# Two heads in alternation on half-filled array tiles, and an ordering model with other costs

## The chip, the cores and the metric

One core of one Trainium2 chip. The metric is device time in microseconds (us) of one execution; the kernel before has a median of 3313.85 us over 3 runs (3313.74 to 3313.91). TensorE (PE) multiplies, VectorE (DVE), ScalarE (ACT) and GpSimd (POOL) work on rows of 128 partitions, SyncE (SP) issues transfers. PEld is TensorE's weight load, which overlaps with its products.

## The reference

512 tokens of width 1024 pass through two blocks of two layers each. The first block's layer: RMS norm, one input projection, two attentions side by side, gated sum, output projection, and a gated FFN. Windowed attention (stage A below): 8 query heads of width 64 in 2 kv groups, query blocks of 128 tokens against a band of the neighbouring blocks, a sink column in the softmax. Neighbourhood attention (stage B): 8 heads on an 8 x 64 grid, query blocks of 16 grid columns against 32.

```python
scores = einsum('bnqkgd,bnjkd->bnkgqj', qb, kb) * HEAD_DIM ** -0.5     # windowed, 4 heads g to one kv head k
p = softmax(concatenate([where(valid, scores, NEG), sink_col], -1))[..., :-1]
out = einsum('bnkgqj,bnjkd->bnqkgd', p, vb)
...
scores = einsum('brjqhd,brjwkhd->bhrjqwk', qg, kb) * HEAD_DIM ** -0.5  # neighbourhood
p = softmax(scores + bias)
out = einsum('bhrjqwk,brjwkhd->brjqhd', p, vb)
```

The second block has retention, a gated linear recurrence and a convolution as mixers, a convolutional FFN and layer norms; no line of its computation is edited.

## The kernel before, in words

Every operand that needs float32 precision is held as a high and a low part in a short format (tiles `hi`, `lo`, and `whi`, `wlo` for weights), and a product is three: hi x hi, lo x hi, hi x lo into the same PSUM tile (`mm3`, line 658; `proj_a` 664 and `proj_b` 680 for weights, 128x512 each, tile `ps`). Attention weights `pe` and values `va` are multiplied in plain float32.

The program is first recorded on virtual tiles (`Recorder.add`, line 349): each operation with its tiles, its predecessors and the engines that may do it. Most have one; `any_tt` may go to VectorE or GpSimd, `any_copy` to ScalarE or VectorE. `order` (line 408) is a list scheduler: it keeps a clock for each engine, takes the first operation in program order that is ready within a window of 3000, prices it by `_cost` (line 289), makes its successors ready a fixed `HOP` of 0.25 us after its end on another engine, and gives a two-way operation to the engine that would end it sooner. Tiles come from lanes with a fixed number of slots; lane `p` is the 8 banks of PSUM. A free slot can be taken again `HOP` after its last use. `issue` (line 581) then issues the operations to the engines' queues in that order, so each queue is what the model made it, and all instructions carry line 603.

In stage A, `attn_a_block` (line 897) runs over one block of 128 queries: for each of the two kv heads, four score tiles `s` (one for each query head of the group; the head width of 64 fills partitions 0 to 63 or 64 to 127, `pr`), the mask and maximum on VectorE, the exponentials on ScalarE, the scaling on VectorE, then per key block four transposes into `pt`, a copy `pe`, and the value product into the rows `pr` of the one output tile `o`, which means 64 of the array's columns. Its four blocks have 2, 3, 3 and 2 key blocks. In stage B, `attn_b_block` (line 984) runs over four blocks of grid columns and four pairs of heads; the two heads of a pair have one row half each. The copies there are `peb` and, of the values, `vb`; the transposes are `ptb` and `vtp`.

The layer norms of the second block (`ln_start` to `ln_end`, lines 1192 to 1233) sum tiles by `any_tt`: `lns`, `lnq`, and `x` times its row factor `spread`.

Of the kernel before, what the change touches and what calls it, by code (L numbers as in the profile page):

```python
# [18 lines left out]
P = 128  # L19
# [18 lines left out]
# ---------------------------------------------------------------- host layout  # L38

def _units_a(w, cols):  # L40
    """Column tiles of w as stationary blocks: [tile, 128, K/128 * 128]."""
    k = w.shape[0] // P
    out = []
    for c in cols:
        out.append(w[:, c].reshape(k, P, len(c)).transpose(1, 0, 2).reshape(P, -1))
    return np.stack(out)


def _units_b(w, cols):
    """A group of columns of w as moving blocks: [unit, 128, kk * len(cols)], 1024 wide."""  # L50
# [161 lines left out]
HOP = 0.25  # L212
# [20 lines left out]
class View:  # L233
    """A tile, a stand-in with its shapes, and the steps that lead to the view from the tile."""
# [19 lines left out]
    def box(self):  # L254
        """Partitions and range of the free dimensions; a whole tile in PSUM."""
# [21 lines left out]
class Op:  # L277
    __slots__ = ("i", "prio", "ways", "args", "kw", "tiles", "new", "npred", "succ", "ready", "done", "start", "cost", "urgent", "columns")
# [10 lines left out]
def _cost(eng, name, args, kw):  # L289
    """Microseconds that the engine is held."""  # L290
    out = kw["out"] if "out" in kw else args[0]
# [11 lines left out]
    if eng == "ACT":  # L303
        return (0.051 if ps else 0.093) + 0.093 * aps + n * 0.000833 + (0.05 if "accum_out" in kw else 0)
    if eng == "POOL":
        return 0.146 + n * 0.00211
# [22 lines left out]
class Recorder:  # L329
# [19 lines left out]
    def add(self, ways, name, args, kw):  # L349
# [5 lines left out]
        if "out" not in kw and isinstance(args[0], View):  # L355
# [17 lines left out]
        ins += [v for v in (args if "out" in kw else args[1:]) if isinstance(v, View)]  # L373
# [23 lines left out]
        if ways == ("PE",):  # L397
            op.columns = outs[0].size * (2 if name == "transpose" else 1 if args[2].ap.dtype == F32R else 4)
# [8 lines left out]
    # -- the order  # L407
    def order(self):
# [30 lines left out]
        def safe(t):  # L439
            """The rest can still run in program order when t takes a slot now."""  # L440
# [30 lines left out]
        while n_sched < len(ops):  # L471
# [17 lines left out]
            while avail[e]:  # L489
# [15 lines left out]
                wait, hold = now, None  # L505
                for t in op.new:
# [3 lines left out]
                    if not sl or not safe(t):  # L510
                        hold = t.lane
                        break
                    wait = max(wait, sl[0])
# [23 lines left out]
            else:  # L537
# [6 lines left out]
                if e == "PE":  # L544
# [3 lines left out]
                    rows = op.args[1].shape[0]  # L548
                    clock[tick] = clock.get(tick, 0.0) + op.columns * rows / P
# [4 lines left out]
            for sp, data in op.succ:  # L554
                same = len(sp.ways) == 1 and sp.ways[0][0] == e
                sp.ready = max(sp.ready, fin + (HOP if not same else SAME if data and e != "PE" else 0.0))
# [3 lines left out]
            for t in op.tiles:  # L560
                t.left -= 1
                t.busy = max(t.busy, fin)
                if t.left == 0 and t.lane in LANES:
                    live[t.lane].discard(t)
                    heapq.heappush(slots[t.lane], t.busy + HOP)
# [15 lines left out]
    def issue(self, tc, order):  # L581
        nc = tc.nc
        engs = {"PE": nc.tensor, "ACT": nc.scalar, "DVE": nc.vector, "POOL": nc.gpsimd, "SP": nc.sync}
        with ExitStack() as ctx:
# [8 lines left out]
            with tc.manual_schedule():  # L593
                for op, e, name, kw in order:
# [7 lines left out]
                    r = lambda v: v.resolve() if isinstance(v, View) else v  # L602
# [1073 lines left out]
```

## Time and profile before

| | |
|---|---|
| median of 3 runs | 3313.85 us (3313.74 to 3313.91) |
| the profiled execution's span | 3312.1 us; its time is this and about 1.75 us around it, by the median of the runs |
| TensorE busy | 3265.5 us, 99%, 16096 instructions |
| VectorE, ScalarE, GpSimd busy | 2117.9 (64%), 1203.7 (36%), 178.2 (5%) us |
| granted TensorE clock | full in all 40 slices of the page |

A row of the timeline with x2 holds two instructions of one kind that start together or one behind the other; the duration is from the first start to the last end. Ends of products are modelled and reach beyond the next start, since products are pipelined: what one costs is the distance between starts. The chip's row names a tile without its number: `s` is any score tile.

### The profile page before, as it was taken

The page shows a single profiled execution, that of the slowest core. Times are in us where ns is not written, and L with a number is a line of the kernel's source. Part 1 is how long each engine was busy: PE and PEld are TensorE (multiplying, and loading weights), DVE is VectorE, ACT ScalarE, POOL GpSimd, SP SyncE. Part 2 cuts the span into 40 slices and gives each one's busy share as a digit, 9 for nine tenths or more (in the row PEclk, how much of TensorE's full clock was granted, in tenths as well). Part 3 has the DMA queues.
Part 4 walks back from the last instruction along what each step waited for, and adds up shares of the span by engine and source line. Part 5 has one row for each costly group of instructions (what it writes and reads, how often), then busy time and mean ns, then how long its engine had stood idle before and what let it go on. Part 6 is the DMA issues. An engine that isn't in the chain of part 4 may idle for free.

```text
span 3312.1 us, 41658 instructions
## 1 busy us (share of the span) xinstructions
PE 3265.5 (99%) x16096; PEld 2701.6 (82%) x16096; DVE 2117.9 (64%) x4317; ACT 1203.7 (36%) x1947; POOL 178.2 (5%) x142
## 2 busy tenths in 40 slices
PE   8999999999999999999999999999999999999998
PEld 6778888887778888888888888888888788888887
DVE  8777766646655544349984457664599954576644
ACT  5543332224543333223332335442333322354431
POOL 1000000000000000000020001000100200010000
PEclk9999999999999999999999999999999999999999
DMA  4345556641133322332212222233232122322331
GB/s 140 112 155 185 197 180 195 187 143 52 64 115 102 95 96 94 94 104 91 83 58 82 90 89 90 96 95 94 73 103 84 56 81 91 96 83 96 96 92 61
DMA packets 99414, 347.16 MB, mean 105 GB/s; under 512 B 11280, under 2 KB 14224, under 8 KB 99216
## 3 DMA queue, kind: packets, MB, share of 16 engines
q1 hardware_dynamic: 99216, 344.51, 32.6%
q8 instruction: 126, 2.06, 0.3%
q14 instruction: 72, 0.59, 0.1%
HBM read 342.36 MB, written 2.10 MB: 104 GB/s over the span
## 4 chain that ended last, share of the span: by engine, by line
PE 93%; DVE 5%; ACT 1%; issue 0%; DMA 0%; POOL 0%; SPq 0%; DVEq 0%; ACTq 0%; POOLq 0%
PE ps L603 87%; PE hs L603 1%; PE o L603 1%; PE s L603 1%; DVE x L603 1%; DVE wlo L603 1%; PE pt L603 1%; DVE scb L603 0%; PE ho L603 0%; PE ro L603 0%; ACT scb L603 0%; PE rs L603 0%; DVE cacc L603 0%; DVE rs_t L603 0%; DVE hw L603 0%
## 5 line engine op out<-in xcount | busy, mean ns | idle before, releaser
L603 PE MATMUL ps<-hi,whi 128*128 128x512 f32 (+1 forms) x3852 | 1466.8, 381 | 4.2 <-ACT hi L603 2.1
L603 PE MATMUL ps<-hi,wlo 128*128 128x512 f32 (+1 forms) x3852 | 1464.6, 381 | 0.8 <-DVE wlo L603 0.8
L603 PE MATMUL ps<-lo,whi 128*128 128x512 f32 (+1 forms) x3852 | 1464.7, 380 | 0.4 <-POOL lo L603 0.4
L603 ACT CAST whi<-raw 128x1024 fp32r<-128x1024 f32 (+1 forms) x540 | 561.2, 1040 | 1442.4 <-PE ps L603 1030.7
L603 DVE TENSOR_TENSOR wlo<-raw,whi 128x1024 fp32r<-128x1024 f32 (+1 forms) x540 | 658.1, 1220 | 553.5 <-ACT whi L603 541.9
L603 PEld LDWEIGHTS ps<-hi,whi 128*128 128x128 f32 x3852 | 726.6, 189 | 140.0 <-ACT whi L603 3.6
L603 PEld LDWEIGHTS ps<-lo,whi 128*128 128x128 f32 x3852 | 728.0, 189 | 134.0 <-issue 1.4
L603 PEld LDWEIGHTS ps<-hi,wlo 128*128 128x128 f32 x3852 | 728.0, 189 | 133.4 <-DVE wlo L603 1.0
L603 PE MATMUL ps<-whi,hi 128*128 128x512 f32 (+1 forms) x512 | 198.0, 388 | 9.4 <-ACT whi L603 9.4
L603 PE MATMUL ps<-wlo,hi 128*128 128x512 f32 (+1 forms) x512 | 197.4, 386 | 0.0
L603 PE MATMUL ps<-whi,lo 128*128 128x512 f32 (+1 forms) x512 | 197.3, 385 | 0.0
L603 DVE SCALAR_TENSOR_TENSOR cacc<-cu,vez,cacc 128x511 f32<-128x511 f32 (+21 forms) x240 | 165.6, 733 | 0.3
L603 DVE TENSOR_TENSOR g<-ps,spread 128x512 f32<-128x512 f32 x76 | 52.5, 691 | 154.7 <-PE ps L603 152.0
L603 DVE CUSTOM_DVE_ANT_0 raw<-raw,cond 128x512 f32<-128x512 f32 x192 | 128.1, 696 | 9.6 <-DMA raw<-in_wada 9.6
L603 DVE SCALAR_TENSOR_TENSOR cv<-ps,vez,cv 128x510 f32<-128x510 f32 (+1 forms) x176 | 130.2, 745 | 2.7
L603 PEld LDWEIGHTS ps<-whi,hi 128*128 128x128 f32 x512 | 97.1, 190 | 29.0 <-ACT whi L603 9.4
L603 PEld LDWEIGHTS ps<-whi,lo 128*128 128x128 f32 x512 | 97.3, 190 | 18.8 <-issue 1.3
L603 PEld LDWEIGHTS ps<-wlo,hi 128*128 128x128 f32 x512 | 97.4, 190 | 18.1 <-issue 1.0
L603 DVE TENSOR_TENSOR t<-ps,spread 128x512 f32<-128x512 f32 x44 | 30.4, 692 | 113.8 <-PE ps L603 113.8
L603 DVE SCALAR_TENSOR_TENSOR g<-g,ps 128x512 f32<-128x512 f32 x80 | 55.0, 687 | 47.3 <-PE ps L603 46.9
L603 POOL TENSOR_TENSOR lnq<-lnq,lsq 128x512 f32<-128x512 f32 (+1 forms) x22 | 40.0, 1819 | 735.6 <-ACT lsq L603 735.5
L603 ACT ACTIVATE hi<-g 128x512 fp32r<-128x512 f32 x76 | 48.1, 633 | 86.4 <-DVE g L603 80.6
(310 smaller groups left out, 2892.1 us busy)
## 6 DMA issues: line engine op xcount, KB each, us to landing
raw<-in_wada SPq DMA_DIRECT2D x96, 512.0 KB, 4.1
raw<-in_wup SPq DMA_DIRECT2D x88, 512.0 KB, 3.7
raw<-in_wgt SPq DMA_DIRECT2D x48, 512.0 KB, 3.7
raw<-in_wg SPq DMA_DIRECT2D x44, 512.0 KB, 3.8
raw<-in_wu SPq DMA_DIRECT2D x44, 512.0 KB, 3.8
raw<-in_wo SPq DMA_DIRECT2D x32, 512.0 KB, 3.7
raw<-in_wd SPq DMA_DIRECT2D x32, 512.0 KB, 3.6
raw<-in_wdn SPq DMA_DIRECT2D x32, 512.0 KB, 3.5
```

The source lines that it names most:

```text
L603: getattr(engs[e], name)(*[r(a) for a in op.args], **{k: r(v) for k, v in kw.items()})
```

## The change

Two things. First, a recorded operation `group`: several products as one unit in the scheduler's eyes, issued one behind the other, with the members of two lists taken in turn (`side`, `mm3s`). Score products and value products of two heads become such groups in `attn_a_block` and `attn_b_block`: the two heads stand on different row halves (scores) or column halves (values) of the array. In `attn_a_block` all eight score tiles of a block are now made first, then both softmaxes, and per key block both kv heads' transposes and copies come before the pair of value products. A group may take several PSUM slots at once. Second, the scheduler's numbers: `HOP` by the engine that ends and `TO` by the one that starts, `SLOT` for the reuse of a slot, other costs of PE, ACT and POOL. Comments and docstrings are removed. What is computed stays the same.

```diff
-HOP = 0.25
+HOP = {"PE": 0.21, "ACT": 0.14, "DVE": 0.13, "POOL": 0.1, "SP": 0.05}
+TO = {"PE": 0.06, "ACT": 0.0, "DVE": 0.0, "POOL": 0.11, "SP": 0.05}
+ACCUM = 0.1
+SLOT = 0.25
+LOAD = 0.1113
...
-            return 0.11
+            return LOAD
...
-            return max(n, cols) / 2400 + 0.003
-        return 4 * max(n, cols) / 2400 + 0.006
+            return max(n / 2400 + 0.0134, LOAD)
+        return 2 * max(2 * n / 2400 + 0.002, LOAD * cols / P)
...
-        return 0.146 + n * 0.00211
+        return 0.15 + n * 0.0029
...
+                    if name == "group":
+                        for a in op.args:
+                            nc.tensor.matmul(*[r(x) for x in a[:3]], start=a[3], stop=a[4])
+                        continue
...
+    def side(self, groups, cost):
+
+        self.r.tensor.group(*[m for ms in zip(*groups) for m in ms], cost=cost)
+
+    def mm3s(self, out, ahi, alo, bhi, blo):
+        return [(out, ahi, bhi, True, False), (out, ahi, blo, False, False), (out, alo, bhi, False, True)]
...
+        for g in range(4):
+            s = [self.ps([P, nk], "s") for _ in range(2)]
+            self.side([self.mm3s(s[kv], *[a[pr, t * P:(t + 1) * P] for a in qT[g]],
+                                 *[a[pr, kbs[0] * P:kbs[0] * P + nk] for a in kT])
+                       for kv, pr in enumerate(heads)], 3 * max(nk / 2400 + 0.0134, 2 * LOAD))
...
-                pt = self.ps(name="pt")
-                for g in range(4):
-                    r.tensor.transpose(pt[:, g * P:(g + 1) * P], sc[g][:, j * P:(j + 1) * P], self.ident)
-                pe = self.m(name="pe")
-                v.any_copy(pe, pt)
-                r.tensor.matmul(o[pr, :], va[:, kb, pr], pe, start=(j == 0), stop=(j == len(kbs) - 1))
...
+        for j, kb in enumerate(kbs):
+            pes = []
+            for kv in range(2):
...
+                pes.append(pe)
+            self.side([[(o[pr, :], va[:, kb, pr], pes[kv], j == 0, j == len(kbs) - 1)]
+                       for kv, pr in enumerate(heads)], 4 * S / 2400 + 0.43)
```

Groups stand at line 630 of the changed kernel, everything else at 632. The issue order moves at three places of the first layer. Names carry a running number: `s_773` is the score tile of one head, and the two operands behind the arrow are the query's and the key's part.

TensorE's queue at the scores of the first query block of stage A, before: `s_773` is a head of the first kv group, `s_788` and `s_794` are heads of the second.

```order
L603 MATMUL s_773<-hi_739,hi_603 128x256
L603 MATMUL s_773<-lo_755,hi_603 128x256
L603 MATMUL s_773<-hi_739,lo_628 128x256
L603 MATMUL ps_639<-wlo_536,hi_151 128x512
L603 MATMUL ps_639<-whi_436,lo_168 128x512
L603 MATMUL ps_649<-whi_436,hi_151 128x512
L603 MATMUL ps_649<-wlo_536,hi_151 128x512
L603 MATMUL s_788<-hi_739,hi_576 128x256
L603 MATMUL s_788<-lo_755,hi_576 128x256
L603 MATMUL s_788<-hi_739,lo_593 128x256
```
After, at the first of these scores: `s_744` is a head of the first kv group, `s_745` of the second, and so are `s_756` and `s_757`.

```order
L630 MATMUL s_744<-hi_727,hi_568 128x256
L630 MATMUL s_745<-hi_727,hi_568 128x256
L630 MATMUL s_744<-lo_735,hi_568 128x256
L630 MATMUL s_745<-lo_735,hi_568 128x256
L630 MATMUL s_744<-hi_727,lo_584 128x256
L630 MATMUL s_745<-hi_727,lo_584 128x256
L630 MATMUL s_756<-hi_727,hi_577 128x256
L630 MATMUL s_757<-hi_727,hi_577 128x256
```
What stood head by head here, with projections between the two kv groups, now stands product by product in turn.

TensorE's queue at the value products of the second query block, before: `o_1047` is the block's output tile; `pe_1024`, `pe_1043`, `pe_1053` are the weights of the first kv group, the other three of the second.

```order
L603 MATMUL o_1047<-pe_1024,va_616 64x512
L603 MATMUL o_1047<-pe_1043,va_616 64x512
L603 MATMUL o_1047<-pe_1053,va_616 64x512
...
L603 MATMUL ps_626<-whi_517,lo_200 128x512
L603 MATMUL o_1047<-pe_1077,va_616 64x512
L603 MATMUL o_1047<-pe_1088,va_616 64x512
L603 MATMUL o_1047<-pe_1093,va_616 64x512
L603 MATMUL s_1109<-hi_739,hi_603 128x384
```
After: `o_1145` is the same block's output; of each pair the first stands for the first kv group.

```order
L632 MATMUL pt_1133<-ident_106,sc_932 128x128
L630 MATMUL o_1145<-pe_1090,va_617 64x512
L630 MATMUL o_1145<-pe_1130,va_617 64x512
L630 MATMUL o_1145<-pe_1094,va_617 64x512
L630 MATMUL o_1145<-pe_1138,va_617 64x512
L630 MATMUL o_1145<-pe_1098,va_617 64x512
L630 MATMUL o_1145<-pe_1150,va_617 64x512
L630 MATMUL s_1167<-hi_727,hi_595 128x384
```
The value products, which came in two runs of three, one kv group each, now come in one run of three pairs.

TensorE's queue at the first scores of stage B, before: the two heads of the first pair as two blocks of three.

```order
L603 MATMUL s_1900<-hi_1777,hi_1542 128x256
L603 MATMUL s_1900<-lo_1785,hi_1542 128x256
L603 MATMUL s_1900<-hi_1777,lo_1550 128x256
L603 MATMUL s_1906<-hi_1777,hi_1542 128x256
L603 MATMUL s_1906<-lo_1785,hi_1542 128x256
L603 MATMUL s_1906<-hi_1777,lo_1550 128x256
```
After: the same six products in turn.

```order
L630 MATMUL s_1900<-hi_1775,hi_1448 128x256
L630 MATMUL s_1901<-hi_1775,hi_1448 128x256
L630 MATMUL s_1900<-lo_1782,hi_1448 128x256
L630 MATMUL s_1901<-lo_1782,hi_1448 128x256
L630 MATMUL s_1900<-hi_1775,lo_1471 128x256
L630 MATMUL s_1901<-hi_1775,lo_1471 128x256
```
Here the same six products stand next to each other in both orders, and only their turn changes.

## Rows read from the trace of the kernel before

**Rows 1.** the page's summary: busy time, share of the span, instructions
```profile
span 3312.1 us, 41658 instructions
...
PE 3265.5 (99%) x16096; PEld 2701.6 (82%) x16096; DVE 2117.9 (64%) x4317; ACT 1203.7 (36%) x1947; POOL 178.2 (5%) x142
```

**Rows 2.** the page's chain that ended last, share by engine
```profile
PE 93%; DVE 5%; ACT 1%; issue 0%; DMA 0%; POOL 0%; SPq 0%; DVEq 0%; ACTq 0%; POOLq 0%
```

**Rows 3.** stretches: length, busy us (instructions) by engine, granted clock, DMA share, GB/s
```profile
61.56:172.20 110.64, 110.63 (x523) 78.45 (x523) 84.32 (x299) 60.35 (x155) 0.00 (x0) 1.00 0.32 101
172.20:199.00 26.80, 24.15 (x240) 17.73 (x239) 25.40 (x124) 20.39 (x72) 0.00 (x0) 1.00 0.43 136
212.00:720.00 508.00, 508.00 (x2251) 420.83 (x2250) 336.52 (x628) 155.41 (x196) 8.16 (x5) 1.00 0.57 183
786.80:895.80 109.00, 109.00 (x523) 78.03 (x522) 68.40 (x239) 55.60 (x143) 0.00 (x0) 1.00 0.12 39
895.80:922.70 26.90, 24.20 (x240) 17.82 (x239) 25.45 (x124) 20.40 (x72) 0.00 (x0) 1.00 0.38 124
```

**Rows 4.** TensorE's timeline, first layer's stage A: start us, us, what
```profile
98.31 0.40 PE L603 MATMUL ps<-wlo,hi 128*128 128x512 f32 x1
98.64 0.39 PE L603 MATMUL s<-hi,hi 64*128 64x256 f32 x1
...
99.54 0.49 PE L603 MATMUL ps<-whi,lo 128*128 128x512 f32 x1
99.97 0.39 PE L603 MATMUL s<-hi,hi 64*128 64x256 f32 x2
...
100.53 0.50 PE L603 MATMUL ps<-whi,hi 128*128 128x512 f32 x1
```

**Rows 5.** the same view, earlier in that stage
```profile
91.63 2.79 PE L603 MATMUL o<-pe,va 128*64 128x512 f32 x6
94.35 0.45 PE L603 MATMUL s<-hi,hi 64*128 64x384 f32 x2
...
94.98 0.33 PE L603 MATMUL s<-hi,hi 64*128 64x384 f32 x1
...
95.60 0.50 PE L603 MATMUL ps<-whi,hi 128*128 128x512 f32 x1
```

**Rows 6.** stretches, of the instructions on the score tiles s alone
```profile
61.56:172.20 110.64, 16.99 (x96) 13.21 (x97) 15.06 (x32) 1.00 0.32 101
786.80:895.80 109.00, 16.42 (x96) 12.74 (x96) 15.10 (x32) 1.00 0.12 39
```

**Rows 7.** stretches, of the instructions on the output tiles o alone
```profile
61.56:172.20 110.64, 18.88 (x40) 4.82 (x40) 3.80 (x16) 3.45 (x16) 1.00 0.32 101
786.80:895.80 109.00, 18.02 (x40) 4.60 (x40) 3.72 (x16) 3.35 (x16) 1.00 0.12 39
```

**Rows 8.** TensorE's timeline, second layer's stage A
```profile
838.43 1.93 PE L603 MATMUL o<-pe,va 128*64 128x512 f32 x6
840.29 0.66 PE L603 MATMUL pt<-ident,sc 128*128 128x128 f32 x4
```

**Rows 9.** VectorE's groups in 61.56:172.2: busy us, mean ns, idle before
```profile
L603 DVE COPY pe<-pt 128x512 f32<-128x512 f32 x5 | 3.4, 687 | 1.1 <-PE pt L603 1.1
```

**Rows 10.** TensorE's timeline, second layer's stage B
```profile
895.82 0.39 PE L603 MATMUL s<-hi,hi 64*128 64x256 f32 x2
896.04 0.29 PE L603 MATMUL s<-lo,hi 64*128 64x256 f32 x2
```

**Rows 11.** weight loads' waits in 172.2:199: us in total, times, longest
```profile
PEld ptb L603 <- DVE scb L603: 2.7, 6, 0.9
```

**Rows 12.** stretches at a layer norm of the second block, one of three
```profile
2369.00:2376.00 7.00, 4.07 (x32) 3.58 (x30) 6.73 (x9) 5.10 (x10) 5.76 (x5) 1.00 0.38 118
2376.00:2382.80 6.80, 5.92 (x27) 5.92 (x28) 6.67 (x29) 2.77 (x7) 0.82 (x1) 0.50 0.33 112
```

**Rows 13.** GpSimd's groups in 1990:2940
```profile
L603 POOL TENSOR_TENSOR x<-x,spread 128x256 f32<-128x256 f32 x9 | 12.7, 1426 | 17.3 <-DVE spread L603 12.3 <-ACT spread L603 5.0
```

More of the change, by code (lines that the diff above doesn't have):

```diff
@@ L277 @@
 class Op:
-    __slots__ = ("i", "prio", "ways", "args", "kw", "tiles", "new", "npred", "succ", "ready", "done", "start", "cost", "urgent", "columns")
+    __slots__ = ("i", "prio", "ways", "args", "kw", "tiles", "new", "npred", "succ", "ready", "done", "start", "cost", "urgent", "columns", "rows")
 def _meet(a, b):
@@ L354, in add @@
         outs = [kw[k] for k in ("out", "accum_out") if isinstance(kw.get(k), View)]
-        if "out" not in kw and isinstance(args[0], View):
+        if name == "group":
+            views = [v for a in args for v in a[:3]]
+            outs = [a[0] for a in args]
+        elif "out" not in kw and isinstance(args[0], View):
             outs.append(args[0])
@@ L372, in add @@
         ins = [v for k, v in kw.items() if isinstance(v, View) and k not in ("out", "accum_out")]
-        ins += [v for v in (args if "out" in kw else args[1:]) if isinstance(v, View)]
+        if name == "group":
+            ins = [v for a in args for v in a[1:3]]
+        else:
+            ins += [v for v in (args if "out" in kw else args[1:]) if isinstance(v, View)]
         if name == "copy_predicated":
@@ L397, in add @@
         if ways == ("PE",):
-            op.columns = outs[0].size * (2 if name == "transpose" else 1 if args[2].ap.dtype == F32R else 4)
+            op.rows = (args[0] if name == "group" else args)[1].shape[0]
+            if name == "group":
+                op.columns = sum(a[0].size * (1 if a[2].ap.dtype == F32R else 4) for a in args) / 2
+            else:
+                op.columns = outs[0].size * (2 if name == "transpose" else 1 if args[2].ap.dtype == F32R else 4)
         op.tiles = list(al.values())
@@ L509, in order @@
                     sl = slots[t.lane]
-                    if not sl or not safe(t):
+                    k = sum(x.lane == t.lane for x in held)
+                    if len(sl) <= k or not safe(t):
                         hold = t.lane
                         break
-                    wait = max(wait, sl[0])
+                    wait = max(wait, heapq.nsmallest(k + 1, sl)[k] if k else sl[0])
+                    held.append(t)
+                    live[t.lane].add(t)
+                for t in held:
+                    live[t.lane].discard(t)
                 if hold is not None:
@@ L547, in order @@
                         cost *= 2
-                    rows = op.args[1].shape[0]
-                    clock[tick] = clock.get(tick, 0.0) + op.columns * rows / P
+                    clock[tick] = clock.get(tick, 0.0) + op.columns * op.rows / P
                 fin = start + cost
@@ L555, in order @@
                 same = len(sp.ways) == 1 and sp.ways[0][0] == e
-                sp.ready = max(sp.ready, fin + (HOP if not same else SAME if data and e != "PE" else 0.0))
+                if same:
+                    hop = SAME if data and e != "PE" else 0.0
+                else:
+                    hop = HOP[e] + TO[sp.ways[0][0]] + (ACCUM if "accum_out" in kw else 0.0)
+                sp.ready = max(sp.ready, fin + hop)
                 sp.npred -= 1
@@ L564, in order @@
                     live[t.lane].discard(t)
-                    heapq.heappush(slots[t.lane], t.busy + HOP)
+                    heapq.heappush(slots[t.lane], t.busy + SLOT)
                     lst = by_lane[t.lane]
@@ L926, in attn_a_block @@
             for g in range(4):
[L927 removed]
+                r.scalar.activation(out=sc[kv][g], in_=sc[kv][g], func=AF.Exp, scale=rs[:, g:g + 1],
                                     bias=nm[:, g:g + 1], accum_out=den[:, g:g + 1])
@@ L1017, in attn_b_block @@
             v.any_copy(pe, pt)
[L1018 to L1023 removed]
+            self.side([[(o[b * HD:(b + 1) * HD, j * P:(j + 1) * P],
+                         vA[vt[kb]][:, (2 * j + b) * HD:(2 * j + b + 1) * HD],
+                         pe[:, (b * 2 + kb) * P:(b * 2 + kb + 1) * P], kb == 0, kb == 1) for kb in range(2)]
+                       for b in range(2)], 8 * LOAD / 2)
         c0 = jb * 16
```

45 lines of the change are left out of this document (20 added, 25 removed).

## The prediction, on record before the changed kernel ran

> **What bounds the kernel now.** I read the page first. TensorE is busy for 3265.5 of 3312.1 us, 99%, and VectorE for 64% [rows 1]; the chain that ended last is TensorE for 93% of its length and VectorE for 5% [rows 2]. So a microsecond taken off TensorE's own work is a microsecond off the kernel, unless VectorE is late at that place. The table by stretches then shows where the edited code stands: the windowed attention (stage A) of the two layers at 61.56:172.2 and 786.8:895.8, and the front of the neighbourhood attention (stage B) at 172.2:199 and 895.8:922.7 [rows 3]. In A TensorE never idles (110.63 of 110.64) and VectorE is at 76% and 63%. In B it is the other way round: VectorE is busy for 25.40 of 26.80 us, TensorE for 24.15. The yardstick of all ordinary work is its line 212:720, 2251 products of 128x512 in 508.00 us: 0.226 us each.
>
> **Part 1: the scores of stage A.** A score product has 64 contraction rows and so uses half of the array. The rows of the timeline give two prices. Between 98.64 and 99.54 six products of one half, 128x256, take 0.90 us. Between 99.97 and 100.53 six products stand, in the lines marked x2, as three pairs of the two halves, and take 0.56 [rows 4]: three products' time is saved, 0.34/3 = 0.113 each. A run of twelve has three pairs more and takes 0.56 + 0.34 = 0.90. For 128x384 the run 94.35 to 95.60 has three pairs (0.63 us, to 94.98) and then three single products (0.62) [rows 5]: six in pairs take about 0.72 with the edge behind them.
> Before: TensorE's score time in A is 16.99 us in the first layer and 16.42 in the second, 96 products each [rows 6]. The issue order puts them in 15 and 14 runs, and each run's last end lies some 0.07 us behind the next instruction's start (99.34 + 0.28 against 99.54), so 15.94 and 15.44 lie on the path. After: both layers have three runs of twelve and two of six of the 128x256 kind and eight runs of six of the 128x384 kind, all in pairs: 3 x 0.90 + 2 x 0.56 + 8 x 0.72 = 9.6. Saved: 6.3 and 5.8.
>
> **Part 2: the value products of stage A.** Each is 128 rows by 64 columns, half of the array's columns, in plain float32, and stands as two passes in the trace (20 products, 40 records [rows 7]). Six passes one behind the other take 94.35 - 91.63 = 2.72 us [rows 5]. At one place the last product of one kv head is followed by the first of the other, and six passes take 840.29 - 838.43 = 1.86 [rows 8]: two of the six went beside two others. So a slot is (2.72 - 1.86)/2 = 0.43 and a run has 2.72 - 6 x 0.43 = 0.14 on top. Before: 40 slots and 8 runs, 17.2 + 1.12 = 18.3, which is the 18.88 of rows 7 less the tails; the second layer's 18.02 less its tails is 17.5. After: 20 slots, in 5 and 4 runs: 8.6 + 0.7 = 9.3 and 9.2. Saved: 9.0 and 8.3.
>
> **Part 3: the edges.** Where the array goes from full to half products or back, a product takes more than 0.226: 0.33 with one such edge behind it (98.31 to 98.64), 0.43 with one on each side (99.54 to 99.97) [rows 4]: 0.10 each. In the issue orders stage A has 42 and 40 such edges before and 28 in each layer after: 26 x 0.10 = 2.6 saved. With these prices, 253 full products and 133 transposes at 0.11, the first layer's stage adds up to 110.5 of the traced 110.64, so nothing large is missing.
> Parts 1 to 3: 6.3 + 5.8 + 9.0 + 8.3 + 2.6 = 32.0 us of TensorE time that nothing hides.
>
> **Part 4: what is late next in A.** The stage shrinks to about 94 us, and VectorE's 84.32 and 68.40 us of work grow a little: of the copies of transposed weights the new order gives it 15 in the two layers where it had 10, 0.69 us each [rows 9], some 1.7 us a layer. So it stands at 92% in the first layer and 75% in the second. All eight score tiles of a block are now made before the first softmax, and a value pair waits for two copies where a product waited for one; behind that wait on TensorE's queue stand the next projections and, through them, the next scores. Cover is there: the new order draws projection products forward into the stage (141 and 140 of them stand between its first score and its last value product, where 55 and 48 did). If the waits come through, the bound is B, where VectorE at 95% leaves TensorE 2.65 of 26.8 us idle, 10% [rows 3]: 0 to 8 us for the first layer. I take 2.5 + 0.5 = 3.0 lost, near the lower end, since TensorE lost nothing in A at 76%.
>
> **Part 5: stage B.** The diff alternates two heads here too, but the trace of before has them side by side already: the order issues three products of one head and then three of the other, and the timeline shows hi,hi of both at 895.82 and lo,hi of both at 896.04 [rows 10]. So alternation as such buys nothing here. What waits in B is the transpose behind VectorE's scaled scores, 2.7 us in 6 waits [rows 11], and the new order puts two large copies out of PSUM per layer, the 0.69 us kind, on ScalarE that were VectorE's. Bounds: all of TensorE's 2.65 idle us per layer, or as much again lost; I take 2 gained each, 4.0, nearer to the gain because VectorE, which holds the stage up, has less to do.
> Here a rule is weighed. The rows show two heads' products starting together though they were queued as blocks. The Trainium skill, TensorE: Matmul & The Clock Gate, Part 3 ("The mechanism"), says that only weight loads are pulled ahead and that matmuls start and end in strict order; by it blocks would run one after the other, and alternation would halve the 96 score products of B as well. By the rows B gains nothing there. I go by the rows and keep the rule as a rival.
>
> **Part 6: the rest.** The model's new costs (GpSimd dearer, waits between engines shorter) re-order everything behind. GpSimd loses 64 additions, VectorE gets 54 instructions, ScalarE 10; DMA issues on the sync queue move with the order, and no DMA is on the chain [rows 2]. It can matter at the three layer norms of the second block: at the one shown TensorE idles 2.93 us while GpSimd is busy 5.76, and then runs 6.8 us at a granted clock of 0.50, the 1.2 GHz level [rows 12]; one 128x256 addition takes GpSimd 1426 ns [rows 13]. But VectorE, which now does these, is busy 6.73 of those 7.00 us itself. Bounds: three times 2.93 + 3.4 gained, 19 us, or 2 us lost at each, 6. I take 3.0 gained, one idle spell out of three.
>
> Sum: -32.0 + 3.0 - 4.0 - 3.0 = -36.0 from the span of 3312.1 gives 3276.1; the profiled execution's time is its span plus 1.75 us to the median of the runs, 3313.85, so the forecast is 3278 us. Its own range, with parts 4 to 6 a few us either way, is 3268 to 3292.
>
> **Rivals.**
> 1. VectorE becomes the bound in A. For it: 92% busy in the first layer, against 95% in B where TensorE does wait. Against: the forward-drawn projections, and 75% in the second layer. Price: 8 us at the first layer and 5 at the second, part 5's gain gone: 3278 + 10 + 4 = 3292, or more with the stage wholly bound, 3290 to 3303. (The Trainium skill, TensorEngine Tiling (Array Packing), "PSUM Bottleneck", warns that packing speeds TensorE and not the copies out of PSUM; the 76% and 95% agree with the direction.)
> 2. The layer norms lose their waits and half-clock spells altogether. For it: GpSimd's 5.76 busy us end just before the clock is back at half. Against: VectorE is full there. Time: 3278 - 16 = 3262, with half of it 3270; 3258 to 3268.
> 3. Products do run strictly in queue order, and B's doubling was something else. B's 96 products per layer are 16 sixes, 16 x 0.34 = 5.4 us more per layer off: 3267. Against it: rows 10.
> 4. The pairing does not do what it says: heads in alternation do not run side by side in A. Then only edges change, some 2.6 to 9 us: 3305 to 3311. Against it: rows 4 and 8.
> 5. Slower: TensorE waits more behind VectorE at the start of B, and its clock falls to the 0.50 level through the whole front of B, in both layers. Then 24.15 and 24.20 us of work take 48 each against 26.8, 21.5 more per layer: 43, against a gain of 32: with part 5's gain gone too, 3313.85 + 43 - 32 = 3325. It decides from some 32 us of full-clock work at half clock. For it: the clock fell at the norm after TensorE had been busy 4.07 of 7.00 us (58%). Against: in B it was busy 90% with the clock at 1.00, and part 5 takes work off VectorE.
>
> **How the numbers follow.** Forecast 0.72, rival 1 0.13, rival 2 0.06, rival 3 0.03, rival 4 0.03, rival 5 0.03. Below 3262 and above 3296 I leave about 0.2: half of rivals 1 and 2, rivals 4 and 5, and the edges of the forecast's own range. No change means within 0.2%, 6.6 us, 3307.2 to 3320.5, about what a measurement of this kernel can tell: half of rival 4 and a third of rival 5, 0.03. Faster: 0.94; slower 0.03.
>
> **What would show it.** Score time in A near 10 us by the same view, value time near 10, and the stage near 94 us per layer; single score products gone from A's timeline, x2 everywhere. B within 2 us of 24.8 per layer. VectorE's busy share in A's first layer near 92% with TensorE's idle time under 3 us. At the norms, the number of half-clock stretches between 2000 and 2935 (three now) tells rival 2. I am wrong if value products of the two heads stand one behind the other, or if idle TensorE time in A exceeds 8 us, or if the time outside A and B moves by more than 10.

## The result and the profile after

The changed kernel took 3282.27 us (median of 4 runs, 3280.33 to 3282.52) against 3313.88 for the kernel before: 31.6 us less, a ratio of 0.9905 with a 95% interval of 0.9893 to 0.9916. The forecast was 3278, its range 3262 to 3296. Measured three more times, four executions each, the same kernel had medians of 3277.34, 3280.41 and 3279.76; over all 16 executions the median is 3280.1, from 3275.3 to 3282.5.

The page's summary after:

```profile
span 3280.7 us, 41593 instructions
...
PE 3236.2 (99%) x16096; PEld 2679.1 (82%) x16096; DVE 2112.6 (64%) x4371; ACT 1205.2 (37%) x1955; POOL 105.4 (3%) x78
```

Against [rows 1], TensorE has 29.3 us less of busy time and the span is 31.4 us shorter; VectorE is where it was, GpSimd has 78 instructions for 142. The chain after:

```profile
PE 88%; DVE 9%; ACT 1%; issue 1%; POOL 0%; DMA 0%; SPq 0%; DVEq 0%; ACTq 0%; POOLq 0%
```

VectorE's share of it rose from 5% [rows 2] to 9%. The stretches, cut at the first score of a layer's stage A, at the first score of stage B and at the end of its last value product (columns as in [rows 3]), after:

```profile
0.00:58.62 58.62, 48.42 (x260) 41.02 (x260) 50.57 (x160) 31.95 (x52) 4.08 (x9) 1.00 0.50 171
58.62:155.26 96.64, 96.36 (x526) 70.14 (x525) 82.95 (x298) 56.51 (x153) 0.00 (x0) 1.00 0.37 120
155.26:192.48 37.22, 35.88 (x328) 26.12 (x328) 32.90 (x152) 30.61 (x99) 0.00 (x0) 1.00 0.52 171
767.60:863.36 95.76, 94.87 (x521) 69.32 (x520) 68.98 (x241) 53.18 (x139) 0.00 (x0) 1.00 0.13 44
863.36:900.59 37.23, 35.89 (x329) 26.14 (x328) 34.14 (x168) 30.61 (x99) 0.00 (x0) 1.00 0.51 171
```

and the three stretches of the kernel before that [rows 3] does not have in this cut:

```profile
0.00:61.56 61.56, 49.93 (x264) 42.64 (x264) 52.41 (x150) 32.08 (x52) 14.54 (x17) 0.97 0.49 164
172.20:212.01 39.81, 37.16 (x328) 26.97 (x327) 35.06 (x156) 30.14 (x96) 0.00 (x0) 1.00 0.51 169
895.82:935.63 39.81, 37.11 (x327) 27.00 (x326) 36.29 (x173) 30.09 (x96) 0.00 (x0) 1.00 0.49 160
```

Stage A shrank from 110.64 to 96.64 and from 109.00 to 95.76 us, all of B from 39.81 to 37.22 and 37.23, the time before the first score from 61.56 to 58.62. The clock was not full there before, although the page's row of tenths shows no dip: its mean is 0.97 in 0.00:61.56 before and 1.00 in 0.00:58.62 after. VectorE stands at 82.95 of 96.64 us in the first stage A, 86%, and TensorE idles there for 0.28 us, in the second for 0.89. The scores alone (the second line is stage B before, the others are after), and the output tiles alone:

```profile
58.62:155.26 96.64, 11.08 (x96) 7.30 (x96) 14.33 (x32) 1.00 0.37 120
172.20:212.01 39.81, 10.06 (x96) 7.42 (x96) 12.60 (x32) 1.00 0.51 169
155.26:192.48 37.22, 8.72 (x96) 6.64 (x96) 12.50 (x32) 1.00 0.52 171
767.60:863.36 95.76, 11.07 (x96) 7.30 (x96) 14.30 (x32) 1.00 0.13 44
```

```profile
58.62:155.26 96.64, 9.69 (x40) 2.42 (x40) 3.71 (x16) 3.31 (x16) 1.00 0.37 120
767.60:863.36 95.76, 9.46 (x40) 2.52 (x40) 3.91 (x16) 3.53 (x16) 1.00 0.13 44
```

Read against [rows 6] and [rows 7]: scores 16.99 to 11.08 and 16.42 to 11.07 us, values 18.88 to 9.69 and 18.02 to 9.46. Stage B's scores went from 10.06 to 8.72 us. In the timeline after (start, us, instruction) every line of scores in stage A is a pair:

```profile
58.62 0.39 PE L630 MATMUL s<-hi,hi 64*128 64x256 f32 x2
...
59.53 0.50 PE L632 MATMUL ps<-whi,lo 128*128 128x512 f32 x1
...
60.66 0.39 PE L630 MATMUL s<-hi,hi 64*128 64x256 f32 x2
...
61.77 0.50 PE L632 MATMUL ps<-whi,hi 128*128 128x512 f32 x1
...
87.14 2.79 PE L630 MATMUL o<-pe,va 128*64 128x512 f32 x12
89.86 0.44 PE L630 MATMUL s<-hi,hi 64*128 64x384 f32 x2
...
91.71 0.76 PE L630 MATMUL s<-hi,hi 64*128 64x256 f32 x2
...
```

The twelve products from 58.62 to 59.53 take 0.91 us, as priced from [rows 4]. The next twelve, from 60.66 to 61.77, take 1.11, and the six from 91.71 to 92.63 take 0.92 where others take 0.56: the price is not the same everywhere. The six value products of a block (twelve passes) take 2.72 us, from 87.14 to 89.86; before, three did [rows 5].

Where the 31.4 us of span came from, in the cut of these views, with the forecast's terms:

| stretch | before | after | moved | forecast |
|---|---|---|---|---|
| to the first score | 61.56 | 58.62 | -2.9 | none |
| stage A, both layers | 219.64 | 192.40 | -27.2 | -32.0 + 3.0 |
| stage B, both layers | 79.63 | 74.44 | -5.2 | -4.0 |
| between the layers' attentions | 574.81 | 575.12 | +0.3 | none |
| all behind the second attention | 2376.47 | 2380.11 | +3.6 | -3.0 |

### The profile page after: what moved, and what is told of

It reads as the page before. It is cut to its first block, busy times and chain, and to the rows that moved or that the text cites. A ratio compares the mean times of both kernels' runs of the same rounds, so it can differ in the third digit from the quotient of the medians.

```text
span 3280.7 us, 41593 instructions
## 1 busy us (share of the span) xinstructions
PE 3236.2 (99%) x16096; PEld 2679.1 (82%) x16096; DVE 2112.6 (64%) x4371; ACT 1205.2 (37%) x1955; POOL 105.4 (3%) x78
## 4 chain that ended last, share of the span: by engine, by line
PE 88%; DVE 9%; ACT 1%; issue 1%; POOL 0%; DMA 0%; SPq 0%; DVEq 0%; ACTq 0%; POOLq 0%
PE ps L632 82%; DVE cacc L632 2%; PE hs L632 1%; DVE wlo L632 1%; PE o L630 1%; DVE x L632 1%; PE s L630 1%; PE pt L632 1%; PE ho L632 0%; DVE lo L632 0%; PE ptb L632 0%; PE ro L632 0%; DVE hw L632 0%; PE rs L632 0%; DVE rs_t L632 0%
## 5 line engine op out<-in xcount | busy, mean ns | idle before, releaser
L632 DVE CUSTOM_DVE_ANT_0 raw<-raw,cond 128x512 f32<-128x512 f32 x192 | 126.6, 686 | 69.4 <-DMA raw<-in_wada 69.2
L632 DVE SCALAR_TENSOR_TENSOR cacc<-cu,vez,cacc 128x487 f32<-128x487 f32 (+19 forms) x240 | 165.0, 733 | 0.3
```

Of the source, the lines that this page charges most:

```text
L632: getattr(engs[e], name)(*[r(a) for a in op.args], **{k: r(v) for k, v in kw.items()})
```

## The experiments

Two theories stood against each other: P, the pairs carry the gain and the scheduler's numbers cost a little; N, the numbers carry a good part of it. The same cut of every trace, the time being the median of its runs (stages of both layers added):

| run | time | to first score | A | B | between | behind |
|---|---|---|---|---|---|---|
| before | 3313.9 | 61.6 | 219.6 | 79.6 | 574.8 | 2376.5 |
| after | 3282.3 | 58.6 | 192.4 | 74.4 | 575.1 | 2380.1 |
| after, three controls | 3277.3, 3280.4, 3279.8 | 57.7, 57.9, 57.6 | 192.4 each | 74.5 each | 575.1, 575.2, 575.2 | 2376.7, 2380.1, 2378.5 |
| groups, old numbers | 3283.0 | 62.7 | 188.6 | 82.3 | 571.7 | 2375.9 |
| numbers only | 3319.7 | 56.5 | 222.5 | 82.5 | 577.6 | 2380.6 |
| blocks | 3278.1 | 57.7 | 192.5 | 74.8 | 575.1 | 2373.9 |
| A's values by head | 3299.5 | 57.4 | 211.1 | 74.5 | 575.2 | 2381.2 |
| A's scores by head | 3293.2 | 57.1 | 206.7 | 76.6 | 573.8 | 2380.0 |
| B ungrouped | 3290.5 | 58.1 | 192.4 | 79.8 | 578.8 | 2380.6 |
| old GpSimd price | 3285.5 | 65.6 | 191.9 | 74.5 | 577.8 | 2376.2 |
| old waits | 3278.5 | 62.4 | 193.2 | 77.6 | 573.5 | 2369.8 |
| old waits in block 2 | 3271.9 | 57.7 | 192.4 | 74.5 | 575.2 | 2370.5 |

Where stage B's first score is issued depends on the order, so a kernel that starts B early has a short A and a long B.

**Groups with all the old numbers.**

```diff
-HOP = {"PE": 0.21, "ACT": 0.14, "DVE": 0.13, "POOL": 0.1, "SP": 0.05}
-TO = {"PE": 0.06, "ACT": 0.0, "DVE": 0.0, "POOL": 0.11, "SP": 0.05}
-ACCUM = 0.1
+HOP = {"PE": 0.25, "ACT": 0.25, "DVE": 0.25, "POOL": 0.25, "SP": 0.25}
+TO = {"PE": 0.0, "ACT": 0.0, "DVE": 0.0, "POOL": 0.0, "SP": 0.0}
+ACCUM = 0.0
...
-        return 0.15 + n * 0.0029
+        return 0.146 + n * 0.00211
```

The costs of TensorE and ScalarE go back too.

> The changed kernel with the groups of two heads kept and all the scheduler's old numbers back (one waiting time of 0.25 us between engines, old costs). Theory P (the pairs carry the gain, the numbers cost a little): block 1 keeps its gain, block 2 goes back to what it was, which in the traces of the two kernels is 5 us better, so 3277 us (3273 to 3281). Theory N (the new numbers carry a good share of the gain, by better placed work around the attention): 3290 us or more.

3282.97 us, ratio to before 0.9907 (0.9891 to 0.9924). N is out: nearly the whole gain is there without a new number. P's own figure, 3277, and its range to 3281 were missed as well: the stretch behind the second attention is shorter as it said (2375.9), but the start went back to 62.7 and A, between and B together are 0.5 us longer than after (842.6 against 842.0).

**Numbers alone, no groups.**

In the kernel before, with the costs of TensorE, ScalarE and GpSimd as in the change:

```diff
-HOP = 0.25
+HOP = {"PE": 0.21, "ACT": 0.14, "DVE": 0.13, "POOL": 0.1, "SP": 0.05}
+TO = {"PE": 0.06, "ACT": 0.0, "DVE": 0.0, "POOL": 0.11, "SP": 0.05}
+ACCUM = 0.1
```

> The kernel before with only the scheduler's new numbers, no groups. Theory P: block 2 loses 5 us, block 1 wins 0 to 4: 3314 to 3319 us. Theory N: 3304 us or less, as part of the gain comes without any pair.

3319.7 us, ratio 1.0018 (1.0008 to 1.0027), slower by 6: P's range was just missed at its upper end, N is out by 16 us. The numbers by themselves shorten the start by 5 us and lengthen everything else.

**Blocks in place of alternation, same order of units.**

```diff
-                        for a in op.args:
+                        for a in op.args[0::2] + op.args[1::2]:
```

> The changed kernel in the very same order of units, but inside a group of scores the three products of one head are issued before the three of the other (no alternation; groups of the A values have one product of each head and don't change). Theory Q, from the rows of before in stage B (blocks of three of two heads stood side by side): no change, 3281 to 3284 us, the score time of A stays at 10.2 us a layer. Rival, matmuls keep strictly to the queue's order: each six of scores takes the single price, 32 sixes in A by 0.34 (128x256) and 0.52 (128x384) or some 7 us a layer and 5 us a layer in B: 3306 us.

3278.1 us, below theory Q's 3281 to 3284 for a reason that the repeated measurements below show; the rival's 3306 is far off. Stage by stage it is the changed kernel: A 192.5 against 192.4, B 74.8 against 74.4. Its scores in the first layer's A and B:

```profile
57.70:154.38 96.68, 11.14 (x97) 7.57 (x97) 14.38 (x32) 1.00 0.36 120
154.38:191.79 37.41, 8.83 (x96) 6.96 (x96) 12.58 (x32) 1.00 0.50 170
```

11.14 and 8.83 us against 11.08 and 8.72. So the turn of the scores is worth 0.1 us a stage; that the two heads are one unit in the queue does it. B is 0.2 us a layer longer, and its value products, which stand in blocks too, take 10.01 us for 9.79. The value products of A, one of each head to a group, do not change in this run, so blocks were not tried for them.

**A's value products by head.**

```diff
-        for j, kb in enumerate(kbs):
-            pes = []
-            for kv in range(2):
+        for kv, pr in enumerate(heads):
+            for j, kb in enumerate(kbs):
...
-            self.side([[(o[pr, :], va[:, kb, pr], pes[kv], j == 0, j == len(kbs) - 1)]
-                       for kv, pr in enumerate(heads)], 4 * S / 2400 + 0.43)
+                r.tensor.matmul(o[pr, :], va[:, kb, pr], pe, start=(j == 0), stop=(j == len(kbs) - 1))
```

> The changed kernel with the value products of stage A by kv head again (all key blocks of one head, then of the other, each by itself for the scheduler), scores still in groups. Theory P: the value time goes back from 18.5 to some 35 us over both layers, 17 more, and a few edges: 3299 to 3303 us. Rival (VectorE bounds the stage now, so TensorE's value time lies beside it): under 3292.

3299.5 us. The first layer's stage, and the output tiles in it:

```profile
57.39:164.12 106.73, 106.71 (x526) 71.96 (x525) 83.08 (x297) 58.50 (x154) 0.00 (x0) 1.00 0.33 109
```

```profile
57.39:164.12 106.73, 19.52 (x40) 4.57 (x40) 3.91 (x16) 3.55 (x16) 1.00 0.33 109
```

9.8 us more of value time and a stage longer by 10.1; 18.7 us over both layers. TensorE idles for 0.02 us in either layer's stage, so nothing hides what the pairs take away.

**A's scores by head.**

```diff
-        for g in range(4):
-            s = [self.ps([P, nk], "s") for _ in range(2)]
-            self.side([self.mm3s(s[kv], *[a[pr, t * P:(t + 1) * P] for a in qT[g]],
-                                 *[a[pr, kbs[0] * P:kbs[0] * P + nk] for a in kT])
...
+        for kv, pr in enumerate(heads):
+            for g in range(4):
...
+                self.mm3(s[kv], *[a[pr, t * P:(t + 1) * P] for a in qT[g]],
+                         *[a[pr, kbs[0] * P:kbs[0] * P + nk] for a in kT], True, True)
```

> The changed kernel with the score products of stage A by kv head again, each tile by itself for the scheduler; value products and stage B stay in groups. Theory P: score time in A goes back from 10.2 to some 15.5 us a layer, 11 us in all: 3291 to 3296 us. Rival (VectorE holds the stage up, so part of it is hidden): under 3288.

3293.2 us. The scores of the first layer's A:

```profile
57.13:161.57 104.44, 15.83 (x96) 12.28 (x97) 14.49 (x32) 1.00 0.32 106
```

15.83 against 11.08; in the second layer 15.56 against 11.07. These 9.2 us, 11 more projection products that the order now puts into the two stages, and 2.1 us more of idle TensorE time make A 14.3 us longer; B is 2.1 longer. The kernel is 11 us slower than the changed kernel's first median and 16 slower than the one measured beside it (3277.3).

**B by single products.**

```diff
-            self.side([self.mm3s(ss[i], *[a[pr, jb * P:(jb + 1) * P] for a in qT[j]],
-                                 *[a[pr, k0:k0 + 256] for a in kT[j]])
-                       for i, pr in enumerate((slice(0, HD), slice(HD, P)))], 6 * LOAD)
...
+                self.mm3(ss[i], *[a[pr, jb * P:(jb + 1) * P] for a in qT[j]], *[a[pr, k0:k0 + 256] for a in kT[j]],
+                         True, True)
```

The value products are single again as well.

> The changed kernel with stage B's scores and values by single products again; stage A stays in groups. Theory G (the group is needed under the new numbers, since without it the order puts transposes between the two heads of a pair, as it did in the run with the numbers alone, whose score time in B was 15.3 and 14.5 us against 9.0): 5 to 6 us a layer lost, 3292 to 3296 us. Rival (the prediction's part 5: B has its overlap without groups): 3280 to 3285.

3290.5 us: theory G's direction, below its range. The first layer's B, and the scores of both layers' B:

```profile
154.70:194.65 39.95, 36.18 (x312) 26.63 (x311) 36.06 (x157) 28.79 (x94) 0.00 (x0) 0.96 0.43 145
```

```profile
154.70:194.65 39.95, 11.90 (x96) 8.56 (x96) 12.66 (x32) 0.96 0.43 145
869.27:909.12 39.85, 11.51 (x96) 8.27 (x96) 12.57 (x32) 1.00 0.47 150
```

One of the four runs, 3284.3, lies in the rival's range, the others don't. B is as long as before the change, 39.95 us, with 11.90 us of scores where the changed kernel has 8.72. The granted clock of 0.96 is not the cause: at 1.00 the second layer has 39.85 and 11.51. B's length alone says too little, since 16 and 13 projection products have left the two layers' B (312 TensorE instructions for 328 in the first), and the stretch between the attentions, where some of them went, is 3.7 us longer. The timeline shows how a pair comes apart:

```profile
166.99 0.38 PE L632 MATMUL s<-lo,hi 64*128 64x256 f32 x1
167.31 0.66 PE L632 MATMUL ptb<-ident,scb 128*128 128x128 f32 x4
167.89 0.38 PE L632 MATMUL s<-hi,lo 64*128 64x256 f32 x1
...
168.12 0.28 PE L632 MATMUL s<-lo,hi 64*128 64x256 f32 x1
168.23 0.27 PE L632 MATMUL s<-hi,lo 64*128 64x256 f32 x1
```

One head's products are spread between transposes and meet a partner only once. The same place in the changed kernel, one after the other:

```profile
165.67 0.39 PE L630 MATMUL s<-hi,hi 64*128 64x256 f32 x2
165.90 0.28 PE L630 MATMUL s<-lo,hi 64*128 64x256 f32 x2
166.01 0.28 PE L630 MATMUL s<-hi,lo 64*128 64x256 f32 x2
```

**GpSimd's old price.**

```diff
-        return 0.15 + n * 0.0029
+        return 0.146 + n * 0.00211
```

> The changed kernel with one number back: GpSimd's old price for an addition, 0.146 + 0.00211 n us. Theory A (GpSimd's price moved both the start, 3 us better, and the gated recurrence of block 2, 4 us worse, by taking additions off GpSimd): the time before the first scores gets 2 to 3 us longer, the stretch of retention and recurrence 4 us shorter, total 3279 to 3283. Rival B (the waits between engines did both): nothing moves in these two places, 3282, or only chance spells of the clock.

3285.5 us, above both theories. The start is 65.6 us long, 8 more than in the controls: theory A's first half, and more than the 2 to 3 that it said. Its waits of TensorE (us in total, times, longest) and its additions on GpSimd:

```profile
PE ps L632 <- DVE acc L632: 2.9, 1, 2.9
```

```profile
L632 POOL TENSOR_TENSOR acc<-acc,sq 128x512 f32<-128x512 f32 x4 | 6.5, 1630 | 12.6 <-DVE lo L632 11.0 <-ACT sq L632 1.5
```

The kernel before has the same wait at the start, with five of its seven additions on GpSimd:

```profile
PE ps L603 <- DVE acc L603: 2.0, 1, 2.0
```

Behind this wait the clock fell to 0.50, the 1.2 GHz level. The same 2 us of 128x512 products in the kernel before and in the changed kernel, which has no such wait (columns as in [rows 3]; in this run it is 0.50 and six products as well):

```profile
25.40:27.40 2.00, 2.00 (x6) 1.56 (x5) 2.00 (x16) 0.14 (x1) 0.00 (x0) 0.50 0.82 252
25.40:27.40 2.00, 2.00 (x10) 1.66 (x9) 1.73 (x7) 0.00 (x0) 0.00 (x0) 1.00 0.06 23
```

At that level these products start 0.43 us apart, at 1.00 they start 0.23 apart. In the changed kernel all seven additions run on VectorE, and wait and spell are gone. The price does not do it alone: with the new price and the old waits (below) two of them are on GpSimd again, TensorE waits 1.6 us, and the start is 62.4 us.

The second half of theory A does not hold. Counted back from its last one, TensorE's products 9100 to 7100 take in retention and gated recurrence of the second block's first layer; the same stretch in the kernel before, the changed kernel and this run:

```profile
1486.41:1875.18 388.77, 387.95 (x2001) 322.68 (x2000) 297.84 (x624) 123.64 (x203) 36.47 (x31) 1.00 0.25 81
1451.08:1843.90 392.82, 390.17 (x2002) 321.60 (x2000) 301.35 (x639) 123.14 (x200) 27.82 (x19) 1.00 0.25 80
1460.67:1853.44 392.77, 390.23 (x2002) 321.72 (x2000) 298.26 (x629) 124.23 (x203) 32.78 (x26) 1.00 0.24 80
```

The 4 us that the change costs here stay with GpSimd's old price.

**The changed kernel again.**

> The changed kernel again, as control beside the others. The run with blocks instead of alternation gave 3278.1 against its 3282.3, and in the traces the two differ at two layer norms only, where the order is the same. Theory C (the clock's half-speed spells at the norms come and go from run to run): this kernel's runs spread over 3276 to 3283. Rival D (blocks are faster than alternation): it stays at 3282 in all runs.

> The changed kernel as control on the same chip as the run beside it: 3276 to 3283 us, by the spread of its two earlier calls (medians 3282.3 and 3277.3).

> The changed kernel as control on the same chip: 3275 to 3283 us, by the spread of its 12 earlier executions.

Theory C holds: the first measurement had a spread of only 2.2 us, but the first control ran from 3275.6 to 3280.5, and rival D's 3282 did not come back. Here are the same three layer norms of the second block (one of them is that of [rows 12]) in three traces: the changed kernel, its first control, and the kernel with blocks, whose second block has the same order.

```profile
1966.00:1988.00 22.00, 17.64 (x108) 17.07 (x107) 20.71 (x68) 13.62 (x30) 1.37 (x2) 0.77 0.20 66
2340.00:2358.00 18.00, 15.27 (x111) 14.66 (x110) 16.55 (x53) 9.74 (x23) 3.11 (x3) 0.91 0.27 89
2888.00:2910.00 22.00, 17.56 (x120) 17.00 (x120) 22.00 (x72) 14.81 (x32) 1.58 (x2) 0.84 0.21 72
```

```profile
1965.30:1987.30 22.00, 17.58 (x130) 17.01 (x129) 21.86 (x71) 15.06 (x34) 1.36 (x2) 0.92 0.19 65
2336.70:2354.70 18.00, 15.11 (x120) 14.21 (x119) 17.37 (x56) 10.72 (x24) 3.10 (x3) 1.00 0.26 89
2883.70:2905.70 22.00, 17.57 (x121) 17.01 (x121) 22.00 (x72) 14.82 (x32) 1.58 (x2) 0.84 0.22 73
```

```profile
1965.70:1987.70 22.00, 17.58 (x131) 17.00 (x130) 21.85 (x71) 15.05 (x34) 1.40 (x2) 0.92 0.20 67
2336.90:2354.90 18.00, 15.10 (x119) 14.20 (x119) 17.36 (x56) 10.64 (x24) 3.12 (x3) 1.00 0.26 89
2884.00:2906.00 22.00, 17.56 (x140) 16.82 (x140) 22.00 (x71) 14.81 (x32) 1.58 (x2) 1.00 0.21 72
```

The granted clock of these stretches is 0.77, 0.91 and 0.84 in the first, 0.92, 1.00 and 0.84 in the second, 0.92, 1.00 and 1.00 in the third. The stretch behind the second attention goes with it: 2380.1, 2376.7 and 2373.9 us. TensorE's waits are the same in all three: 4.3 or 4.4 us in all at the first of these norms, 2.7 or 2.8 at the middle one and its approach, 4.4 at the last. So 6 us of the differences between these runs are half-clock spells that come or don't behind the same waits, and the 4 us by which the blocks seemed faster are of this kind.

The same count from the last product gives the second block in pieces (us; the layers are the second block's, "recurrence" is the stretch with its retention and gated recurrence; between these pieces all traces agree within 0.1):

| products | before | after | three controls | blocks | old GpSimd price | old waits in block 2 | all old numbers |
|---|---|---|---|---|---|---|---|
| 9100 to 7100, first layer's recurrence | 388.8 | 392.8 | 392.8 or 392.9 | 392.9 | 392.8 | 389.9 | 388.8 |
| 6700 to 6300, first norm | 59.6 | 62.3 | 59.7, 62.3, 60.7 | 59.6 | 59.0 | 58.9 | 59.4 |
| 4700 to 4300, middle norm | 72.3 | 70.3 | 69.3, 70.3, 70.3 | 69.3 | 69.6 | 69.2 | 71.6 |
| 4300 to 1900, second layer's recurrence | 468.3 | 468.7 | 468.7 or 468.8 | 468.8 | 470.8 | 466.0 | 469.9 |
| 1900 to 1500, last norm | 64.5 | 65.9 | 65.7 or 65.8 | 63.4 | 62.8 | 64.6 | 63.9 |
| the last 300 and the end | 67.2 | 64.5 | 64.6 or 64.7 | 64.4 | 65.4 | 66.5 | 67.5 |

**The old waits, in all of the kernel and in block 2 alone.**

```diff
-HOP = {"PE": 0.21, "ACT": 0.14, "DVE": 0.13, "POOL": 0.1, "SP": 0.05}
-TO = {"PE": 0.06, "ACT": 0.0, "DVE": 0.0, "POOL": 0.11, "SP": 0.05}
-ACCUM = 0.1
+HOP = {"PE": 0.25, "ACT": 0.25, "DVE": 0.25, "POOL": 0.25, "SP": 0.25}
+TO = {"PE": 0.0, "ACT": 0.0, "DVE": 0.0, "POOL": 0.0, "SP": 0.0}
+ACCUM = 0.0
```

> The changed kernel with the new prices kept, and the old waits back: 0.25 us between any two engines, nothing on top for the reader or for an accumulated output. Theory H (GpSimd's price makes the start better, the waits between engines make the recurrence of block 2 worse): the idle time of TensorE before the first scores stays near 4 us, that of the recurrence's stretch falls from 12.9 to 9, and the kernel is 4 us faster than the changed kernel in the same call. Rival (waits and prices only act together): the recurrence's stretch stays at 12 to 13 and the time within 2 us of the changed kernel.

3278.5 us, 1.9 less than the control beside it, whose runs overlap with it: theory H predicted 4, and the rival's "within 2 us" fits the time as well. The stretch behind is 2369.8 us, 7 to 10 less than in the controls, and the first layer's recurrence takes 389.9 us as theory H's direction asks. But the start (62.4) gives 4.6 back, so waits act there too, not the price alone. Hence the second:

```diff
-                    hop = HOP[e] + TO[sp.ways[0][0]] + (ACCUM if "accum_out" in kw else 0.0)
+                    hop = HOP[e] + TO[sp.ways[0][0]] + (ACCUM if "accum_out" in kw else 0.0) if op.i < self.mark else 0.25
...
+            self.r.mark = len(self.r.ops)
             self.block2(layers2)
```

> The changed kernel with the old wait of 0.25 us between engines for the operations of the second block alone; the first block, the groups and all prices as in the changed kernel. Theory H (the new waits cost the second block some 3 to 8 us of idle TensorE time, and win some in the first): first block as in the changed kernel, second as in the run with the old waits, 4 to 8 us under the changed kernel: 3272 to 3276 us. Rival (the gains come from chance spells of the clock, not from the order): within 2 us of the control beside it.

3271.9 us (3271.8 to 3274.3), ratio to before 0.9878 (0.9862 to 0.9895); the control beside it 3279.8 (3275.6 to 3282.1). The first block is the changed kernel's in every stretch, the rest 2370.5 against 2378.5. Theory H holds, with a time just under its 3272 to 3276. All its runs lie below all 16 of the changed kernel. Of the 8 us against its control's trace 2.9 are won in the first layer's recurrence, 2.7 in the second's and 4.1 at the three norms, spells included, and 1.9 are lost at the end. At the first norm, TensorE's longest waits in this kernel (us in total, times, longest):

```profile
PE ps L633 <- POOL lnq L633: 1.7, 1, 1.7
PE ps L633 <- DVE lo L633: 0.8, 1, 0.8
```

and the changed kernel's, in its timeline (wait in brackets):

```profile
1978.59 0.58 PE L632 MATMUL ps<-lo,whi 128*128 128x256 f32 x1 [3.07 <-DVE lo L632]
```

The changed kernel waits 3.07 us for the low part of an operand that stands on VectorE's queue behind products of `x` with its row factor `spread`: VectorE starts this `lo` at 1978.12 and has put eight of them ahead of it since 1974.86.

## Why the prediction was right, step by step

**What bounds it.** Right. TensorE idles for 0.28 us of the first stage A, and undoing either half of the pairs gave about its product time or more back to the stage: 9.8 and 9.2 us of values made the two layers' A 10.1 and 8.6 longer, 9.2 us of scores made them 14.3 longer together.

**Parts 1 and 2.** The values came out as priced: 9.69 less the tails of 5 runs is 9.3, 9.46 less 4 is 9.2. The scores are 0.6 us a layer dearer than forecast: 11.08 less 13 tails of 0.07 is 10.2 where 9.6 was said, by two of the first layer's thirteen runs: 0.2 us at 60.66 and 0.36 at 91.71; the eight of the 128x384 kind take the 0.72 that was said.

**Parts 3 and 4.** Together they ask for a stage of 93.9 + 2.5 us in the first layer and 93.7 + 0.5 in the second; 96.64 and 95.76 were measured. Rival 1 did not come: VectorE's work in the first layer fell from 84.32 to 82.95 us where 1.7 more were forecast, it stands at 86% and not 92%, and TensorE idles for less than a microsecond a layer. So part 4's loss is about as large as it said in the first layer and not of its kind: of the 2.7 us above 93.9, 0.6 are dearer scores, 0.7 three projection products more (526 instructions for the 523 of [rows 3]) and 0.3 idle time. The rest, 1.1, is part 3's term, which was sized too large: from start to start, and with the count of products allowed for, full products and transposes together came out 0.2 us cheaper in the first layer's stage where 1.4 were forecast, and 0.15 in the second's where 1.2 were. What took the saved edges back is open. (Part 3's check of the stage's time adds up to 110.2 by its own prices, not 110.5.)

**Part 5.** The size, 2.0 a layer for 2.6 measured, was right, and the reason was only half of it. The step that failed is "alternation as such buys nothing here" as it was used: the turn of the products buys next to nothing (blocks: 74.8 against 74.4), but the group is more than alternation. It keeps the scheduler from putting transposes between the two heads, and 2.7 us a layer go when it is taken away. Rows 10 showed the first pair of a stage that stood together, and I took it for all of them: B's scores took 10.06 us before and 8.72 after, so some pairs were apart. Of the 2.59 us in the first layer TensorE's busy time is 1.28 (37.16 to 35.88), which the scores' 1.34 account for, and its idle time 1.31. The idle time is the gain that part 5 did forecast, with VectorE's work down from 35.06 to 32.90; but ungrouping also brought VectorE's busy time back (36.06), so the runs do not part the group's adjacency from the copies that moved with it. Rival 3 is out: the blocks' scores take 11.14 us in A and 8.83 in B, against 11.08 and 8.72 in turn. By the strict order that the Trainium skill states (TensorE: Matmul & The Clock Gate, Part 3, "The mechanism") the blocks would have been slower, and these traces do not agree with it.

**Part 6.** Wrong in sign: 3 us gained were forecast, 0.2 to 3.7 lost in four traces of one kernel. The step that failed is that it priced the three norms alone and put the rest of the second block at nothing. There the first layer's recurrence lost 4.0 us in each of the four traces, and the end of the program won 2.5 to 2.7. The 4.0 come with the new numbers (392.8 us with them and no groups too), 2.9 of them go with the old waits, and GpSimd's price alone changes nothing there. The norms together moved from 2.1 us lost to 1.7 won: taking GpSimd's additions off them was no sure gain, since VectorE, named there as full, then made TensorE wait 3.07 us at the first. Rival 2's spells neither vanished nor grew: there were three half-clock stretches at the norms before, and four, two, three and three in the four traces. What the part left out too is the start, where GpSimd's price and the waits together won 3 to 4 us; the row that shows it (2.0 us of wait for `acc`) was there to be read, and so was the clock behind it. That the sum is within 4.3 us, 3278 against 3282.3 at first and 3280.1 over all, is in part luck: 6.6 us too much behind the second attention and 1.8 in A were offset by 2.9 at the start and 1.2 in B.

Which of the new waits costs the second block is open: taking all of them back wins 8 us there, and they were not taken back one by one. Why a run of six pairs takes 1.11 us at one place and 0.91 at another was not tried either.

## What to carry to other kernels

Score products that use different halves of the array need only stand next to each other in the queue; make them one unit for whatever orders the work, and their turn within it can stay as it is. (For the value products of stage A only the pairing as a whole was tried, not their turn.) Price such a change from runs of the same trace where pairs and singles already occur, and count how many pairs a stage really has before calling it paired. A global table of costs that orders a whole program moves places that have nothing to do with the edit: read the same cut of every stage, and let a table differ by stage where that pays.

## What the runs showed of the hardware

Two heads' score products run side by side when queued as blocks of three (11.14 us of scores) as when queued in turn (11.08). A wait of 2.0 us near the start of the kernel before cost more than itself: behind it 128x512 products started 0.43 us apart at a granted clock of 0.50, where the changed kernel, without the wait, had them 0.23 us apart at 1.00. And the granted clock behind one and the same wait of TensorE differs between executions: 0.77 against 0.92 over 22 us at the first norm and 0.91 against 1.00 over 18 us at the middle one in two executions of the changed kernel, 0.84 against 1.00 over 22 us at the last norm in the changed kernel and the one with blocks, whose second block has the same order; the engine was busy for 17.6, 15.1 to 15.3 and 17.56 to 17.57 us.
